# Moving weight casts and head gating to POOL, and reordering DVE, in the attention stage of a hybrid encoder step

## The chip, the cores and the metric

One core of one Trainium2 chip runs the whole program in a single launch. The metric is the device time of an execution in microseconds, lower is better. Times given for a kernel are the median of several runs; one further execution was taken with the hardware profiler, and every view quoted here is of that execution.

## The reference, cut to what matters

One layer of a streaming encoder works on 1024 prompt frames and 32 sample frames, which the kernel holds together as 1056 columns. The input is RMS-normed and multiplied by one wide matrix, from whose columns come queries, keys, values, forget logits, two gate paths and two mixing gates. Two branches follow and are merged:

```python
q, k, v, lf, ga, u, gb, ma, mb = mixer_inputs(xp, ...)      # one projection, split by columns
c = cumsum(lf)
# attention: 16 heads of 64, blocks of 128 queries
s = q @ k.T + c_q - c_k;  s = where(causal, s, min);  o = softmax(s) @ v
# convolution branch: depthwise width 31, LayerNorm over 1024 channels
conv = dwconv(u)
ya = (o * silu(ga)) @ w_pa
yb = (silu(layernorm(conv)) * silu(gb)) @ w_pb
m  = sigmoid(ma) * ya + sigmoid(mb) * yb
y  = x + m @ w_out
```

The sample frames do the same against a cache of 512 past frames.

## The kernel before, in words

**Stages.** The program goes through five stretches: the x split and first projections, the projections with the convolution running beside them, the attention, the two branch projections (pa, pb) and the output projection. This change lies in the attention. There PE does four kinds of work: the scores of a block, the transposes of the normalised weights P, the products with V, and, as filler between them, the remaining projections of the gates (gb, ma, mb).

**Numbers in halves.** A projection is made of three f16 products: the weight is cast to a high part `wh` (line 138) and a low part `wl` = raw - wh (line 141, three instructions of 3, 3 and 2 eighths of the weight), and the input likewise (`xh`, `xl`). Weights go in batches of two. Their jobs are hung on a counter of ticks: one tick is one step of a projection, three matmuls, and a projection has 24 ticks (8 k-tiles for each of 3 column chunks), so that a batch lasts 48. A batch's jobs, in ticks from the batch before it: squares for the scale (3, 13), the sum by PE (`total`, 25), the power of two (`power`, 27), the cast of each weight (`split`, 29 and 39) and its three low parts (`rest`, one, three and five ticks after the cast). A job that falls due is issued at that place in the engines' queues.

**Attention.** `seq` holds 132 items in order: 16 heads with 8 blocks of 128 queries (block i of a head sees (i+1) x 128 keys), and four `Sample` items. Step n of the main loop issues, in this order: the scores of item n+3 (`start`, which calls `scores`: PE products into `psS`, then on DVE the causal mask, line 1124, and the negated row maximum, line 1126); on some steps DMA loads of the next head; `turn` of item n (PE transposes P through `psT` banks, ACT copies the first four 128-wide pieces, DVE copies the rest when there are more than four, that is for blocks 4 to 7; both are line 1156); `soft` of item n+3 (ACT exponential with row sum, line 1133); `norm` of item n+2 (DVE reciprocal, line 1138, and POOL scaling of P, line 1139); filler ticks; `values` of item n-2 where it is due; filler ticks again. The second call of `values` that matters is at block 7: PE products with V (line 1172), ACT copies one half-row group (line 1176), DVE adds the other (line 1177), and for every second head DVE multiplies by the gate `ga` (line 1179), which a DMA brings (line 1161). The result goes to memory through SP (line 1181).

**Buffers.** `psS` has two buffers, so the scores of item n+3 wait for the exponential of item n+1. `psT` has two banks shared by transposes, value products, LayerNorm sums and the batch sums: a transpose waits until the copy of an earlier one has emptied a bank. `wh` and `wl` turn over three buffers, `raw` over four.

**Order.** In the attention the queues of PE, SP, DVE and ACT are as written in the program (`manual_schedule`); that of POOL is put in order by a planner with its own costs and due times.

**Fillers.** `fill(n)` issues n ticks of the remaining projections. Every step has two calls of `fill(2)`, but the first three blocks of head 8 have none. 22 projections, 528 ticks, are issued so. The LayerNorm statistics (`layernorm`) also run one piece a step once the convolution's sums are there, which in the profile is about head 8.

Of the kernel before, what the change touches and what calls it, by code (L numbers as in the profile page):

```python
# [8 lines left out]
F32 = mybir.dt.float32  # L9
# [5 lines left out]
ALU = mybir.AluOpType  # L15
# [38 lines left out]
def build(tc, xT, xt, wv, wf, ckT, cv, clT, stT, vec, cst, yT, kT, vO, lfO, cpT, csT):  # L54
# [35 lines left out]
    class Batch:  # L90
# [44 lines left out]
            nc.gpsimd.tensor_scalar(self.inv, q, back, 1.0, op0=ALU.mult, op1=ALU.mult)  # L135

        def high(self, i, wh, raw, ks):
            nc.scalar.mul(wh[:, ks, :], raw[:, ks, :], self.s[:, i:i + 1])  # L138

        def low(self, i, wl, wh, raw, ks):  # L140
# [80 lines left out]
    def begin():  # L221

        if not plan:
            return
        b = plan.pop(0)
        after = plan[0] if plan else None
        t = pace["tick"]
        jobs = [(25, b.total), (27, b.power)]
        if b.keys[0] == ("v", 0):
            jobs = [(32, b.total), (33, b.power), (10, lambda: b.stage(0)), (17, lambda: b.stage(1)),  # L230
                    (34, lambda: split.__setitem__(b.keys[0], split_v(0, b)))]
        elif b.n == 2:
            jobs += [(3, lambda: b.stage(0)), (13, lambda: b.stage(1))]
            for i, n in ((0, 29), (1, 39)):
                jobs.append((n, lambda i=i: b.split(i)))
                jobs += [(n + 1 + 2 * p, lambda i=i, p=p: b.rest(i, p)) for p in range(3)]
        else:
            jobs += [(3 + 10 * i, lambda i=i: b.stage(i)) for i in range(2)]
            jobs.append((29, lambda: split.__setitem__(b.keys[0], split_v(b.keys[0][1], b))))
        if after:  # L240
            jobs += [(5 + 10 * i, after.load) for i in range(after.n)]
        prep.extend((t + n, fn) for n, fn in sorted(jobs, key=lambda e: e[0]))
# [115 lines left out]
    def sums(f):  # L358
        return [lambda: from_shift(f, sides["y", f]), lambda: into_sums(f, sides["y", f])]
# [637 lines left out]
    pe = ExitStack()  # L997
    pe.enter_context(tc.manual_schedule(engines={E.PE, E.SP, E.DVE, E.Activation}))
    pace["rate"], pace["credit"] = R_A, 0.0
    taps.extend(sums(7))  # L1000
    psS = pool("psS", 2, stack=p2, space=PS)
    psT = pool("psT", 2, stack=p2, space=PS)
# [20 lines left out]
    def fill(n):  # L1023
        for _ in range(n):
            next(flow, None)

    class Sample:
# [15 lines left out]
        def scores(self):  # L1043
            g, kc, pf = self.g, self.kc, self.pf
            ps = psS.tile([128, 2, 512], F32, name="psS", tag="S")
            for j in range(4):
                rows = slice(64 * (j % 2), 64 * (j % 2) + 64)
                q = qs_t[rows, 2 * g + j // 2, :]
                nc.tensor.matmul(ps[32 * j:32 * j + 32, 0, :], q, kc[rows, j // 2, :], start=True, stop=True)
                nc.tensor.matmul(ps[32 * j:32 * j + 32, 1, :TS], q, ks_t[rows, 2 * g + j // 2, :],  # L1050
                                 start=True, stop=True)
            nc.vector.scalar_tensor_tensor(pf[:, :PAST], ps[:, 0, :], cq[:, g:g + 1], pf[:, :PAST],
                                           op0=ALU.add, op1=ALU.subtract)
# [50 lines left out]
    class Block:  # L1104
# [5 lines left out]
        def scores(self):  # L1110
            i = self.i
            QA, QB, KA, KB = self.head.q
            nk = (i + 1) * 128
            qsl = slice(i * 128, i * 128 + 128)
            ps = psS.tile([128, 2, 512], F32, name="psS", tag="S")
            nb = 1 if nk <= 512 else 2
            w = nk // nb
            wm = max(w, 256)
            for b in range(nb):
                ksl = slice(b * w, b * w + wm)  # L1120
                nc.tensor.matmul(ps[:, b, :wm], QB[:, qsl], KB[:, ksl], start=True, stop=False)  # L1121
                nc.tensor.matmul(ps[:, b, :wm], QA[:, qsl], KA[:, ksl], start=False, stop=True)  # L1122
            diag = ps[:, nb - 1, w - 128:w]
            nc.vector.tensor_add(diag, diag, cmask)  # L1124
            nm = ap.tile([128, 3], F32, name="nm", tag="nm", bufs=6)
            nc.vector.tensor_reduce(nm[:, 0:1], ps[:, :nb, :w], axis=AX.XY, op=ALU.max, negate=True)  # L1126
            self.at = ps, nm, nk, nb, w
# [30 lines left out]
        def values(self):  # L1158
            if self.i == 5 and self.head.h % 2:
                self.head.g = ap.tile([128, T], F32, name="ga", tag="kc", bufs=1)  # L1160
                nc.sync.dma_start(self.head.g, s_g["ga"][self.head.h // 2, :, :T])
            if self.i < 7:
                return
            e, V, ot, parts = self.head.h % 2, self.head.V, self.head.ot, self.head.p
            own = slice(64 * e, 64 * e + 64)
            oth = slice(64 - 64 * e, 128 - 64 * e)
            pos = [psT.tile([128, 512], F32, name="po", tag="T") for _ in range(2)]
            for c in range(4):
                po = pos[c // 2][:, 256 * (c % 2):256 * (c % 2) + 256]
                for j in range(2 * c + 2):  # L1170
                    rows = slice(64 * (j % 2), 64 * (j % 2) + 64)
                    nc.tensor.matmul(po[rows], V[:, j, :], parts[c][:, j, :], start=(c % 2 == 0 and j < 2),  # L1172
                                     stop=(c % 2 == 1 and j >= 2 * c))
            for u in range(2):
                sl = slice(512 * u, 512 * u + 512)
                nc.scalar.copy(ot[own, sl], pos[u][oth])
                nc.vector.tensor_add(ot[own, sl], ot[own, sl], pos[u][own])
                if e == 1:
                    nc.vector.tensor_mul(ot[:, sl], ot[:, sl], self.head.g[:, sl])
            if e == 1:  # L1180
                nc.sync.dma_start(s_o[self.head.h // 2, :, :T], ot)

# [23 lines left out]
    def layernorm():  # L1206

        shift = sides["shift"]
        for _ in range(4):
            yield  # L1210
        yield from over_channels(mean, lambda sl, ps: nc.scalar.mul(mean[:, sl], ps, 1.0 / D))

        def put(sl, ps):
            t = t352("t", 3)
            nc.scalar.activation(t, mean[:, sl], AF.Square)
            nc.vector.scalar_tensor_tensor(rstd[:, sl], ps, 1.0 / D, t, op0=ALU.mult, op1=ALU.subtract)
            nc.vector.tensor_add(mean[:, sl], mean[:, sl], shift[:, sl])
            nc.vector.tensor_scalar(rstd[:, sl], rstd[:, sl], EPS, None, op0=ALU.add)

        yield from over_channels(rstd, put)  # L1220
# [16 lines left out]
    heads[1].load()  # L1237
    for n in range(3):
        start(seq[n])
        seq[n].soft()  # L1240
        if n:
            seq[n - 1].norm()
        fill((8, 4, 0)[n])
    for n, b in enumerate(seq):
        if n + 3 < len(seq):
            start(seq[n + 3])
        if n + 9 < len(seq) and getattr(seq[n + 9], "i", 1) == 0:
            seq[n + 9].head.load()
        if n + 6 < len(seq) and isinstance(seq[n + 6], Sample):
            seq[n + 6].load()  # L1250
        if getattr(b, "i", 0) == 3 and b.head.h + 1 < H:
            heads[b.head.h + 1].load_v()
        b.turn()
        if n + 3 < len(seq):
            seq[n + 3].soft()
        if n + 2 < len(seq):
            seq[n + 2].norm()
        some = 2 if isinstance(b, Sample) or b.i > 2 or b.head.h != 8 else 0
        fill(some)
        if n >= 2 and pending(seq[n - 2]):  # L1260
            seq[n - 2].values()
        fill(some)
        if n >= 3 and isinstance(seq[n - 3], Sample):
            seq[n - 3].finish()
        if "ready" in sides:
            next(ln, None)
# [402 lines left out]
```

## Time and profile before

| what | value |
|---|---|
| time, median of 3 runs | 1348.63 us (1346.65 to 1349.82) |
| the profiled execution: its own time | 1345.89 us |
| the profiled execution: span from first to last instruction | 1344.1 us |
| busy share of the span: PE, DVE, ACT, POOL | 98%, 74%, 53%, 38% |
| chain that ended last: PE, DVE, ACT, issue, DMA | 82%, 9%, 3%, 2%, 2% |
| granted TensorE clock, mean | 0.996 |

A busy PE is a modelled quantity: matmuls overlap, so a row's duration is longer than the distance to the next one. A stall of PE therefore shows only where it is longer than the overlap. A wait is put down to the instruction whose signal came last. The page cuts the span into stretches by time; the attention lies from about 570 to 1055 us.

### The profile page before, as it was taken

What the parts mean: (1) busy time and instruction counts of PE and PEld (TensorE: products, weight loads), DVE (VectorE), ACT (ScalarE), POOL (GpSimd) and SP (SyncE); (2) the same over time, 40 slices, a digit from 0 to 9 for tenths busy, and PEclk for the clock granted to TensorE, in tenths of its full rate; (3) what the DMA queues carried; (4) which work ended last, traced back from release to release, by engine and by line L of the source; (5) the groups of instructions that cost most, each with busy time, mean ns of one, the idle gap of its engine ahead of it and who ended that gap; (6) DMA issues with size and microseconds to landing.
All of it is one profiled execution on the core that took longest, in us unless ns stands there. A gap on an engine that the chain in (4) does not pass through costs nothing.

```text
span 1344.1 us, 24837 instructions
## 1 busy us (share of the span) xinstructions
PE 1312.6 (98%) x9383; PEld 1003.1 (75%) x9383; DVE 990.4 (74%) x1532; ACT 719.0 (53%) x1362; POOL 505.8 (38%) x548
## 2 busy tenths in 40 slices
PE   8999999999999999999889998999999999999999
PEld 5687876666666666667567766777776699999998
DVE  6797879888999997987778866655554489166664
ACT  6644555757676743455555555655555566233320
POOL 2001124547484820243433442222222158255562
PEclk8999999999999999999999999999999999999999
DMA  6343233425352463535644643565452698544462
GB/s 251 98 140 104 93 112 118 139 82 187 95 180 87 162 166 109 160 90 155 165 109 123 186 132 99 147 179 132 131 152 54 240 313 262 176 128 146 142 190 69
DMA packets 113496, 194.97 MB, mean 145 GB/s; under 512 B 34080, under 2 KB 80032, under 8 KB 113376
## 3 DMA queue, kind: packets, MB, share of 16 engines
q1 hardware_dynamic: 113232, 193.31, 46.9%
q8 instruction: 74, 1.21, 0.4%
q14 instruction: 46, 0.38, 0.1%
q10 hardware_dynamic: 144, 0.07, 0.0%
HBM read 127.68 MB, written 65.64 MB: 144 GB/s over the span
## 4 chain that ended last, share of the span: by engine, by line
PE 82%; DVE 9%; ACT 3%; issue 2%; DMA 2%; SPq 1%; POOL 0%; DVEq 0%; ACTq 0%; POOLq 0%
PE pj L183 56%; PE pjv L761 6%; PE pj L1501 6%; PE po L1172 4%; PE ptr L1153 3%; DVE nm L1126 2%; DVE wl L141 2%; DVE y L371 2%; PE psS L1122 2%; PE psS L1121 2%; DMA ga<-s_ga 2%; ACT wh L138 1%; DVE psS L1124 1%; DMA s_q<-qh 1%; PE warm L477 1%
## 5 line engine op out<-in xcount | busy, mean ns | idle before, releaser
L183 PE MATMUL pj<-xh,wh 128*128 128x352 f16 (+2 forms) x1536 | 481.6, 314 | 2.3 <-ACT wh L138 1.4
L183 PE MATMUL pj<-xh,wl 128*128 128x352 f16 (+2 forms) x1536 | 481.2, 313 | 0.7 <-DVE wl L141 0.6
L183 PE MATMUL pj<-xl,wh 128*128 128x352 f16 (+2 forms) x1536 | 480.9, 313 | 0.5 <-DVE xl L579 0.4
L183 PEld LDWEIGHTS <-wh 128*128 128x128 f16 x3072 | 301.5, 98 | 162.1 <-issue 7.1
L371 DVE SCALAR_TENSOR_TENSOR y<-u,vec_t,y 128x1086 f32<-128x1086 f32 x240 | 346.8, 1446 | 12.0 <-ACT y L368 8.9
L1139 POOL TENSOR_SCALAR P<-P,nm 128x128 f32<-128x128 f32 (+7 forms) x128 | 129.9, 1015 | 279.9 <-DVE nm L1138 229.8
L183 PEld LDWEIGHTS <-wl 128*128 128x128 f16 x1536 | 150.5, 98 | 72.0 <-DVE wl L141 1.6
L141 DVE SCALAR_TENSOR_TENSOR wl<-raw,sc,wh 128x384 f16<-128x384 f32 (+1 forms) x192 | 128.2, 693 | 48.3 <-ACT wh L138 48.3
L1133 ACT ACTIVATE P<-psS,nm 128x128 f32<-128x128 f32 (+7 forms) x128 | 95.1, 743 | 113.3 <-DVE nm L1138 70.9
L1126 DVE TENSOR_REDUCE nm<-psS 128x1 f32<-128x128 f32 (+7 forms) x128 | 97.0, 758 | 12.5
L1153 PE MATMUL ptr<-ident,P 128*128 128x128 f32 x576 | 88.6, 276 | 17.3 <-DVE pt L1156 9.2
L175 POOL TENSOR_TENSOR wl<-raw,wh 128x384 fp32r<-128x384 f32 (+1 forms) x51 | 63.3, 1270 | 74.3 <-ACT wh L172 58.6
L1153 PEld LDWEIGHTS ptr<-ident,P 128*128 128x128 f32 x576 | 69.2, 141 | 28.2 <-DVE pt L1156 12.1
L1156 ACT COPY pt<-ptr 128x512 f32<-128x512 f32 (+3 forms) x128 | 64.3, 502 | 44.4 <-PE ptr L1153 43.2
L1121 PE MATMUL psS<-KB,QB 128*128 128x256 f32 (+2 forms) x192 | 81.8, 427 | 0.6 <-ACT P L1133 0.6
L880 POOL TENSOR_TENSOR sql<-sqf,sqh 128x352 fp32r<-128x352 f32 x48 | 57.0, 1187 | 65.8 <-ACT sqh L877 65.8
L138 ACT ACTIVATE wh<-raw,sc 128x1024 f16<-128x1024 f32 (+1 forms) x68 | 73.9, 1091 | 8.2 <-DVE sc L158 7.9
L1172 PE MATMUL po<-pt,V 128*64 128x256 f32 x640 | 72.8, 382 | 2.5 <-ACT pts L1078 1.7
L1124 DVE TENSOR_TENSOR psS<-psS,cmask 128x128 f32<-128x128 f32 x128 | 37.6, 294 | 46.0 <-PE psS L1122 45.6
L906 POOL TENSOR_TENSOR ql<-qn,qh 128x352 fp32r<-128x352 f32 (+1 forms) x48 | 67.8, 1429 | 6.6 <-ACT qh L905 6.5
L761 PE MATMUL pjv<-vwh,xh 128*128 128x260 f16 x256 | 70.1, 274 | 0.0
L761 PE MATMUL pjv<-vwl,xh 128*128 128x260 f16 x256 | 70.0, 273 | 0.0
(271 smaller groups left out, 2532.9 us busy)
## 6 DMA issues: line engine op xcount, KB each, us to landing
raw<-wf SPq DMA_DIRECT2D x92, 512.0 KB
QB<-s_q SPq DMA_DIRECT2D x32, 256.0 KB
KB<-s_k SPq DMA_DIRECT2D x32, 256.0 KB
kT<-qn SPq DMA_DIRECT2D x8, 528.0 KB
s_ga<-t SPq DMA_DIRECT2D x24, 176.0 KB
s_gb<-t SPq DMA_DIRECT2D x24, 176.0 KB
s_ma<-t SPq DMA_DIRECT2D x24, 176.0 KB
s_mb<-t SPq DMA_DIRECT2D x24, 176.0 KB
```

The costliest lines, as they stand in the source:

```text
L138: nc.scalar.mul(wh[:, ks, :], raw[:, ks, :], self.s[:, i:i + 1])
L141: nc.vector.scalar_tensor_tensor(wl[:, ks, :], raw[:, ks, :], self.s[:, i:i + 1], wh[:, ks, :], op0=ALU.mult, op1=ALU.subtract)
L183: nc.tensor.matmul(ps, a[:, kt, :], b(kt, sl), start=(first and n == 0), stop=(last and n == N - 1))
L371: t = nc.vector.scalar_tensor_tensor(y, u[:, i:i + CW], w, y, op0=ALU.mult, op1=ALU.add)
L761: nc.tensor.matmul(ps[:, :VC], a, b, start=(n == 0), stop=(n == 23))
L1121: nc.tensor.matmul(ps[:, b, :wm], QB[:, qsl], KB[:, ksl], start=True, stop=False)
L1126: nc.vector.tensor_reduce(nm[:, 0:1], ps[:, :nb, :w], axis=AX.XY, op=ALU.max, negate=True)
L1133: nc.scalar.activation(P[:, :nk].rearrange("p (b w) -> p b w", b=nb), ps[:, :nb, :w], AF.Exp, bias=nm[:, 0:1], accum_out=nm[:, 1:2])
L1139: nc.gpsimd.tensor_scalar(P[:, :nk], P[:, :nk], nm[:, 2:3], 1.0, op0=ALU.mult, op1=ALU.mult)
L1153: nc.tensor.transpose(pt[:, 128 * j:128 * j + 128], P[:, 128 * (4 * u + j):128 * (4 * u + j) + 128], ident)
L1172: nc.tensor.matmul(po[rows], V[:, j, :], parts[c][:, j, :], start=(c % 2 == 0 and j < 2), stop=(c % 2 == 1 and j >= 2 * c))
L1501: nc.tensor.matmul(pss[c][:, :HC], a[:, k, :], x, start=(not more and kt == 0 and n == 0), stop=(kt == 3 and n == 2), skip_group_check=more)
```

## The change

- While the attention runs, the cast of a weight to `wh` is a POOL `tensor_scalar` instead of an ACT `mul`. A batch begun there has its sum at tick 23 (was 25), its power at 24 (27), its casts at 25 and 34 (29 and 39), and its low parts 6, 8 and 10 ticks behind the cast (was 1, 3 and 5), which puts them at 31, 33, 35 and 40, 42, 44 (was 30, 32, 34 and 40, 42, 44).
- `scores` issues the PE products alone. The mask and the maximum are in a new method `top`, which the main loop calls after `turn`, ahead of `soft`. So DVE's copy of the turned P is issued ahead of the mask and maximum of the item three further on. Sample items are split the same way.
- The product with the gate `ga` is issued on POOL instead of DVE.
- In LayerNorm the ACT square of the mean's chunk is issued one step ahead of the matmul and the DVE work that uses it.
- The first three blocks of head 8 get filler ticks like all others; block 6 of heads 2 to 13 gets three ticks in place of four. The sum of ticks stays 528.

```diff
         def high(self, i, wh, raw, ks):
+            if sides.get("cast") == "pool":
+                nc.gpsimd.tensor_scalar(wh[:, ks, :], raw[:, ks, :], self.s[:, i:i + 1], 1.0, op0=ALU.mult, op1=ALU.mult)
+                return
             nc.scalar.mul(wh[:, ks, :], raw[:, ks, :], self.s[:, i:i + 1])
...
         elif b.n == 2:
             jobs += [(3, lambda: b.stage(0)), (13, lambda: b.stage(1))]
-            for i, n in ((0, 29), (1, 39)):
+            lag = 6 if sides.get("cast") == "pool" else 1
+            for i, n in ((0, 29), (1, 39)) if lag == 1 else ((0, 25), (1, 34)):
                 jobs.append((n, lambda i=i: b.split(i)))
-                jobs += [(n + 1 + 2 * p, lambda i=i, p=p: b.rest(i, p)) for p in range(3)]
+                jobs += [(n + lag + 2 * p, lambda i=i, p=p: b.rest(i, p)) for p in range(3)]
+            if lag > 1:
+                jobs[:2] = [(23, b.total), (24, b.power)]
...
     pace["rate"], pace["credit"] = R_A, 0.0
+    sides["cast"] = "pool"
...
+        def top(self):
+            ps, nk, nb, w = self.at
             diag = ps[:, nb - 1, w - 128:w]
             nc.vector.tensor_add(diag, diag, cmask)
...
                 if e == 1:
-                    nc.vector.tensor_mul(ot[:, sl], ot[:, sl], self.head.g[:, sl])
+                    nc.gpsimd.tensor_mul(ot[:, sl], ot[:, sl], self.head.g[:, sl])
...
-        def put(sl, ps):
+        for c in range(3):
+            sl = csl(c)
             t = t352("t", 3)
             nc.scalar.activation(t, mean[:, sl], AF.Square)
-            nc.vector.scalar_tensor_tensor(rstd[:, sl], ps, 1.0 / D, t, op0=ALU.mult, op1=ALU.subtract)
+            yield
+            pm = psT.tile([128, 512], F32, name="psn", tag="T")
+            nc.tensor.matmul(pm[:, :CH], ones_f, rstd[:, sl], start=True, stop=True)
+            nc.vector.scalar_tensor_tensor(rstd[:, sl], pm[:, :CH], 1.0 / D, t, op0=ALU.mult, op1=ALU.subtract)
...
         b.turn()
         if n + 3 < len(seq):
+            seq[n + 3].top()
             seq[n + 3].soft()
         if n + 2 < len(seq):
             seq[n + 2].norm()
-        some = 2 if isinstance(b, Sample) or b.i > 2 or b.head.h != 8 else 0
-        fill(some)
+        fill(2)
         if n >= 2 and pending(seq[n - 2]):
             seq[n - 2].values()
-        fill(some)
+        fill(1 if getattr(b, "i", 0) == 6 and 2 <= b.head.h < 14 else 2)
```

More of the change, by code (lines that the diff above doesn't have):

```diff
@@ L1051, in scores @@
                                  start=True, stop=True)
+            self.ps = ps
+        def top(self):
+            g, ps, pf = self.g, self.ps, self.pf
             nc.vector.scalar_tensor_tensor(pf[:, :PAST], ps[:, 0, :], cq[:, g:g + 1], pf[:, :PAST],
@@ L1122, in scores, with top @@
                 nc.tensor.matmul(ps[:, b, :wm], QA[:, qsl], KA[:, ksl], start=False, stop=True)
+            self.at = ps, nk, nb, w
+        def top(self):
+            ps, nk, nb, w = self.at
             diag = ps[:, nb - 1, w - 128:w]
@@ L1211, in layernorm @@
         yield from over_channels(mean, lambda sl, ps: nc.scalar.mul(mean[:, sl], ps, 1.0 / D))
-        def put(sl, ps):
+        for c in range(3):
+            sl = csl(c)
             t = t352("t", 3)
             nc.scalar.activation(t, mean[:, sl], AF.Square)
-            nc.vector.scalar_tensor_tensor(rstd[:, sl], ps, 1.0 / D, t, op0=ALU.mult, op1=ALU.subtract)
+            yield
+            pm = psT.tile([128, 512], F32, name="psn", tag="T")
+            nc.tensor.matmul(pm[:, :CH], ones_f, rstd[:, sl], start=True, stop=True)
+            nc.vector.scalar_tensor_tensor(rstd[:, sl], pm[:, :CH], 1.0 / D, t, op0=ALU.mult, op1=ALU.subtract)
             nc.vector.tensor_add(mean[:, sl], mean[:, sl], shift[:, sl])
             nc.vector.tensor_scalar(rstd[:, sl], rstd[:, sl], EPS, None, op0=ALU.add)
-        yield from over_channels(rstd, put)
         for c in range(6):
@@ L1239, in build @@
         start(seq[n])
+        seq[n].top()
         seq[n].soft()
```

## The prediction

> **What bounds the kernel now.** I read the stages by window first, then PE's waits in the attention, then what DVE waits for there, then the timeline around a few stalls.
>
> ```profile
> core 0: us, PE busy (x) PEld busy (x) DVE busy (x) ACT busy (x) POOL busy (x), PEclk, DMA share, GB/s
> 46.00:570.00 524.00, 523.17 (x3750) 363.86 (x3749) 461.81 (x529) 305.60 (x564) 193.31 (x192) 1.00 0.41 130
> 800.00:850.00 50.00, 45.26 (x296) 32.70 (x296) 31.97 (x80) 28.61 (x69) 12.23 (x21) 0.97 0.48 117
> 1055.00:1255.00 200.00, 200.00 (x1266) 193.48 (x1265) 119.69 (x133) 88.39 (x116) 104.94 (x77) 1.00 0.64 213
> 570.00:1055.00 485.00, 463.86 (x3447) 335.10 (x3446) 321.92 (x694) 272.83 (x590) 155.12 (x218) 1.00 0.48 130
> ```
>
> PE is full before the attention (523.17 of 524 us) and after it (200.00 of 200), so only the attention has room: 485.00 - 463.86 = 21.1 us of idle PE. DVE is busy for 321.92 of the 485 us, ACT for 272.83, POOL for 155.12; none is the bound by its work. Who ended PE's idle time:
>
> ```profile
> PE ptr L1153 <- DVE pt L1156: 9.2, 11, 1.7
> PE ptr L1153 <- ACT pt L1156: 6.4, 5, 2.2
> PE po L1172 <- ACT pts L1078: 1.7, 2, 0.9
> PE ptr L1153 <- DVE ot L1177: 1.2, 1, 1.2
> PE po L1172 <- ACT mean L1211: 0.7, 1, 0.7
> PE psS L1121 <- ACT P L1133: 0.6, 2, 0.4
> PE psn L1202 <- ACT pt L1156: 0.6, 1, 0.6
> ```
>
> The columns are us in total, times, the longest. They sum to 20.4 us, nearly all of the idle time, and nearly all is one thing: a transpose waits for a bank of psT that DVE or ACT has not emptied. Both queues are first in, first out, so the question is what stood ahead of the copy. Two stalls:
>
> ```profile
> 648.41 1.22 DVE L1126 TENSOR_REDUCE nm<-psS 128x1 f32<-128x1024 f32 x1
> 649.55 0.28 DVE L1156 COPY pt<-ptr 128x128 f32<-128x128 f32 x1
> 649.89 0.44 PE L1153 MATMUL ptr<-ident,P 128*128 128x128 f32 x2 [1.16 <-DVE pt L1156]
> ```
>
> ```profile
> 679.16 1.14 ACT L138 ACTIVATE wh<-raw,sc 128x1024 f16<-128x1024 f32 x1
> 680.21 0.54 ACT L944 ACTIVATE t<-pj,sc 128x352 f32<-128x352 f32 x1
> 680.34 0.62 DVE L141 SCALAR_TENSOR_TENSOR wl<-raw,sc,wh 128x384 f16<-128x384 f32 x1 [2.19 <-ACT wh L138]
> 680.73 0.58 ACT L1156 COPY pt<-ptr 128x512 f32<-128x512 f32 x1
> 681.37 0.33 PE L1153 MATMUL ptr<-ident,P 128*128 128x128 f32 x1 [1.05 <-ACT pt L1156]
> ```
>
> In the first, a copy of 0.28 us stands behind a maximum of 1.22 us that nobody needs for another step. In the second, ACT's copy stands behind a weight cast of 1.14 us, and DVE meanwhile stood 2.19 us at the low part, which waits for that cast. DVE's own waits say how often:
>
> ```profile
> DVE psS L1124 <- PE psS L1122: 45.6, 48, 2.3
> DVE wl L141 <- ACT wh L138: 32.5, 20, 2.2
> DVE ot L1179 <- DMA ga<-s_ga: 9.9, 6, 3.3
> ```
>
> 20 waits for a cast and 6 for the gate's DMA, 42.4 us, are idle time of DVE with copies and maxima queued behind it.
>
> **The change part by part.** Rows for the prices:
>
> ```profile
> L138 ACT ACTIVATE wh<-raw,sc 128x1024 f16<-128x1024 f32 x22 | 25.1, 1140 | 0.0
> L1179 DVE TENSOR_TENSOR ot<-ot,ga 128x512 f32<-128x512 f32 x16 | 11.1, 693 | 10.2 <-DMA ga<-s_ga 9.9
> L1139 POOL TENSOR_SCALAR P<-P,nm 128x1024 f32<-128x1024 f32 x16 | 21.1, 1317 | 14.7 <-DVE nm L1138 9.9 <-ACT P L1133 4.5
> L175 POOL TENSOR_TENSOR wl<-raw,wh 128x384 fp32r<-128x384 f32 x34 | 45.3, 1354 | 74.3 <-ACT wh L172 58.6 <-issue 15.4 <-POOL ml L1421 0.2
> L351 POOL TENSOR_TENSOR rstd<-rstd,y 128x1024 f32<-128x1024 f32 x7 | 19.0, 2720 | 20.3 <-ACT y L355 20.3
> L371 DVE SCALAR_TENSOR_TENSOR y<-u,vec_t,y 128x1086 f32<-128x1086 f32 x46 | 64.0, 1391 | 2.3 <-ACT y L368 2.2
> L141 DVE SCALAR_TENSOR_TENSOR wl<-raw,sc,wh 128x384 f16<-128x384 f32 (+1 forms) x67 | 39.1, 605 | 32.5 <-ACT wh L138 32.5
> ```
>
> and from the waits and the timeline, with the taps of the first 170 us of the attention by window:
>
> ```profile
> 570.00:740.00 170.00, 49.26 (x35) 1.00 0.47 127
> PEld ptr L1153 <- POOL P L1139: 2.0, 4, 1.2
> 715.49 1.33 DVE L371 SCALAR_TENSOR_TENSOR y<-u,vec_t,y 128x1086 f32<-128x1086 f32 x1
> 715.67 2.14 POOL L1139 TENSOR_SCALAR P<-P,nm 128x1024 f32<-128x1024 f32 x1
> 838.79 1.12 POOL L1139 TENSOR_SCALAR P<-P,nm 128x1024 f32<-128x1024 f32 x1 [0.30 <-DVE nm L1138]
> 836.98 1.52 POOL L1139 TENSOR_SCALAR P<-P,nm 128x896 f32<-128x896 f32 x1 [5.12 <-DVE nm L1138]
> 839.15 0.93 PE L1153 MATMUL ptr<-ident,P 128*128 128x128 f32 x7
> ```
>
> *Casts to POOL, low parts six ticks behind.* ACT loses 22 x 1.14 = 25.1 us. POOL gains 22 instructions of a kind whose nearest row is the scaling of P, also 1024 wide and one tensor in, 1.317 us in the mean: 29 us. No row here writes f16 from POOL, so I keep the ends of the timeline rows, 1.12 and 2.14 us: 25 to 47 us. A batch of 48 ticks is 12 steps of four ticks, about 12 x 485/132 = 44 us, so six ticks are about 5.5 us, over twice the dearer cast; the low parts find it done and DVE's 32.5 us go. On PE this is the ACT row: the copies that wait behind a cast. I take 5 of its 6.4 us; the rest stood behind squares and evacuations that stay.
>
> *Mask and maximum behind the copy.* Only steps that turn blocks 4 to 7 have a DVE copy, so 64 steps change. The copy is then first in line, and 8 of the 9.2 us go (the rest stood behind taps and low parts, which stay). The added wait: the maximum now waits for a copy that waits for up to eight transposes. Seven take 0.93 us (row at 839.15) and the copy 0.28, so the maximum, the exponential on ACT behind it and the reciprocal come about 1.2 us later where DVE was idle, nothing where it was late. They are needed two steps on, about 2 x 485/132 = 7 us, so I cost this at nothing in the sum and keep what it takes from P's margin for the rivals.
>
> *Gate on POOL.* DVE loses 16 x 0.693 = 11.1 us and the 9.9 us of DMA wait. POOL gets 16 products with two tensors in: between 1.354 us for 384 columns and 2.720 for 1024, by the line through both 1.63 us at 512, together 26 us, plus the same DMA wait. What is queued behind on POOL is the next scaling of P. On PE the "DVE ot" row, 1.2 us, goes; the store of `ot` comes some 2 us later, with nothing waiting for it but a buffer two heads on.
>
> *Squares ahead, fillers spread.* Twelve ticks of three matmuls go to head 8:
>
> ```profile
> 491.34 21.50 PE pj L183 x144
> 827.39 0.50 PE L183 MATMUL pj<-xh,wh 128*128 128x352 f16 x1
> 837.12 0.31 PE L183 MATMUL pj<-xh,wh 128*128 128x352 f16 x1
> ```
>
> At 21.50/144 = 0.149 us each that is 12 x 3 x 0.149 = 5.4 us of PE work into a place where PE stood, taken from steps where it did not: the same work, but the LayerNorm waits (0.7 and 0.6 us) are covered. Around 827 us the same matmul took 0.50 us where it takes 0.31 ten us later, and the window 800 to 850 has a clock of 0.97: 0.03 x 50 = 1.5 us, which goes if PE does not thin out there. Each removed wait also hides 0.31 - 0.149 = 0.16 us of a matmul's modelled tail; some 16 waits, 2.6 us.
>
> *New costs.* POOL's three sources together go from 155 to about 155 + 29 + 26 = 210 of 485 us, and its order is a planner's. The weight loads of transposes wait for POOL 2.0 us today. I let that double, and 0.6 us for DVE: 2.6 us. Its ends are 0, if POOL's idle time takes everything, and the 33 us of the slower rival.
>
> **Sum.** 8 + 5 + 1.2 + 1.3 + 1.5 + 2.6 - 2.6 = 17 us. Against the profiled execution: 1345.9 - 17 = 1328.9. That execution lies 2.7 us below the median of the runs, so on their scale 1348.6 - 17 = **1331.6 us**. The most that can go is 21.1 us idle, 1.5 of clock and some 4 of tails (26 waits x 0.16), 27 us: 1322. By a third to a half of the terms missing, 9 us: 1340.
>
> **The rivals.** *The port eats DVE's gain.* At 715.67 the scaling of P started 0.18 us into a tap and took 2.14 us, against 1.12 alone: the two exclude each other. Taps and low parts, 64.0 + 39.1 us of DVE's time, are the instructions with two tensors in. If the 55 us added on POOL held DVE for their whole length, DVE would be as late as with the 32.5 + 9.9 + 11.1 = 53.5 us it gets rid of, and the 8 and 1.2 us would stay lost. Left are 5 + 1.3 + 1.5 and 1 of tails, less 2: 7 us, 1341.6 (1337 to 1346). Against it: the taps end early (35 of the 46 lie before 740 us, 49.26 of 64.0 us), and 103.1 of 485 us of DVE's time, a fifth, is of this kind. The Trainium skill, "SBUF — State Buffer", section "Who interferes with whom", says that a DVE instruction with two SBUF inputs and a GpSimd one that reads SBUF share a port that is locked for the whole instruction, the later one fully blocked; by that rule every such meeting costs the loser its whole wait, and the time would lean to this rival's 1341.6. The rows at 715 agree.
>
> *POOL becomes late (slower).* POOL is in order. Block 6's scaling ended at 836.98 + 1.52 = 838.50 and its transposes began at 839.15: 0.65 us to spare. A cast of 2.14 us ahead of such a scaling costs PE 1.5 us; at all 22 casts 33 us, less the 17: +16, 1364.6. It breaks even when 17/1.5 = 11 of the casts stand before a tight block. For it: POOL's order is a planner's, gate products wait there for DMA, and the later reciprocal takes from the same margin. Against it: POOL idles most of the stage, and a cast is issued behind the scaling of its own step.
>
> *One wait for another (no change).* The maximum is up to 1.2 us later, so the exponential is, and ACT's copy of the next block stands behind the exponential: the 17 us come back as waits for ACT, 1348.6 (1346 to 1351). Against it: ACT has 25.1 us less to do, and had only 273 of 485.
>
> **How the numbers follow.** Forecast 0.64 (1324 to 1340), the port 0.16, POOL late 0.12, no change 0.08. A measurement of this kernel tells 0.2%, 2.7 us. Faster: the forecast and the port, 0.80; same 0.08; slower 0.12. The range runs from 1322, where all is won, to 1350, which leaves out the slower case and little else (some 0.15 above, 0.05 below).
>
> **What would show it.** Right: PE's idle time in the attention falls from 21 us to 4 to 8, "DVE wl <- ACT wh" is gone, the DVE copies' row of PE's waits falls under 2 us, and no clock below 0.99 stands in a window about head 8. POOL's cast takes 1.1 to 2.1 us, its gate product 1.3 to 2.7. Wrong: transposes wait for "POOL P" by more than 5 us (POOL late); low parts and taps grow well above 0.605 and 1.391 us with the copies still late (the port); "ACT pt" grows above 6.4 us (one wait for another).

## Result and the profile after

The changed kernel takes **1331.7 us** in the median (1330.78 to 1332.38), the kernel before 1347.64 us (1345.03 to 1349.82) beside it: ratio 0.9869, 95% interval 0.9851 to 0.9888, or 17.7 us less. The profiled execution took 1331.66 us (span 1329.8, mean clock 0.997).

The attention by window, after, with the stretch about head 8, in the same columns as before:

```profile
800.00:850.00 50.00, 49.97 (x347) 36.06 (x346) 31.45 (x81) 27.83 (x66) 19.74 (x30) 1.00 0.54 140
570.00:1038.00 468.00, 458.29 (x3436) 333.68 (x3434) 315.41 (x678) 248.48 (x568) 211.95 (x254) 1.00 0.50 135
```

The attention now ends at about 1038 us, and PE idles 468.00 - 458.29 = 9.7 us in it, where it idled 21.1. The stretch about head 8 is full (49.97 of 50 us, clock 1.00). By the first and the last instruction of the attention in the chain, the stage went from 482.4 us (570.23 to 1052.64) to 466.8 (571.27 to 1038.09): 15.6 us less. What lies before it took 1.0 us longer and what lies behind it 0.2, so the whole gain is in the attention. The two profiled executions differ by 14.2 us (1345.89 - 1331.66), less than the medians, as that of before lay below its median.

PE's waits there, after (us in total, times, the longest):

```profile
PE po L1187 <- ACT pts L1089: 2.6, 2, 1.8
PE ptr L1168 <- ACT pt L1171: 2.4, 2, 1.7
PE ptr L1168 <- DVE pt L1171: 1.7, 2, 1.4
PE ptr L1168 <- DVE os_t L1113: 1.5, 2, 1.2
PE ptr L1168 <- POOL P L1154: 1.1, 3, 0.6
...
```

The two rows of the turned copies, 9.2 and 6.4 us before, are 1.7 and 2.4 now. Three rows grew: `pts`, which belongs to the four Sample items, `os_t` and POOL's scaling of P; the last two were not in the list.

The queues that changed hands, after: DVE's wait for the cast, and the weight loads that wait for POOL.

```profile
DVE wl L144 <- POOL wh L139: 0.3, 1, 0.3
PEld ptr L1168 <- POOL P L1154: 3.5, 5, 1.5
```

And the two moved operations (count, busy us, mean ns, and POOL's idle time ahead of them with what ended it):

```profile
L139 POOL TENSOR_SCALAR wh<-raw,sc 128x1024 f16<-128x1024 f32 x22 | 24.5, 1126 | 0.0
L1194 POOL TENSOR_TENSOR ot<-ot,ga 128x512 f32<-128x512 f32 x16 | 21.7, 1358 | 32.5 <-DMA ga<-s_ga 15.2 <-DVE ot L1192 14.2 <-issue 3.1
```

DVE's 32.5 us behind the cast are gone (0.3). The gate's DMA wait did not go away: it moved to POOL, where it is longer (15.2 us) and costs PE little: transposes wait 1.1 us for POOL's scaling of P, their weight loads 3.5 us (2.0 before).

### The profile page after: what moved, and what is told of

The parts are those of the page before. It is cut to its first block, busy times and chain, and to the rows that moved or that the text cites. A ratio compares the mean times of both kernels' runs of the same rounds, so it can differ in the third digit from the quotient of the medians.

```text
span 1329.8 us, 24806 instructions
## 1 busy us (share of the span) xinstructions
PE 1308.3 (98%) x9383; PEld 1002.7 (75%) x9383; DVE 979.6 (74%) x1516; ACT 695.2 (52%) x1340; POOL 559.4 (42%) x586
## 4 chain that ended last, share of the span: by engine, by line
PE 89%; DVE 5%; ACT 2%; issue 1%; POOL 1%; DMA 1%; SPq 1%; DVEq 0%; POOLq 0%; ACTq 0%
PE pj L186 60%; PE pjv L767 6%; PE pj L1519 6%; PE po L1187 5%; PE ptr L1168 4%; PE psS L1133 2%; PE psS L1132 2%; DVE wl L144 1%; DVE y L377 1%; DMA s_y<-y 1%; PE pst L866 0%; DVE nm L1141 0%; PE pst L867 0%; DMA ga<-s_ga 0%; PE ptx L582 0%
## 5 line engine op out<-in xcount | busy, mean ns | idle before, releaser
L1154 POOL TENSOR_SCALAR P<-P,nm 128x128 f32<-128x128 f32 (+7 forms) x128 | 143.8, 1124 | 195.2 <-DVE nm L1153 171.6
L144 DVE SCALAR_TENSOR_TENSOR wl<-raw,sc,wh 128x384 f16<-128x384 f32 (+1 forms) x192 | 133.3, 718 | 16.3 <-ACT wh L141 15.8
L178 POOL TENSOR_TENSOR wl<-raw,wh 128x384 fp32r<-128x384 f32 (+1 forms) x51 | 59.6, 1196 | 61.0 <-ACT wh L175 46.4
L120 POOL CAST topb<-tops 128x2 bf16<-128x2 f32 x35 | 19.0, 541 | 137.0 <-ACT junk L117 87.1
L767 PE MATMUL pjv<-vwh,xl 128*128 128x260 f16 x256 | 69.9, 273 | 0.0
```

The costliest lines, as they stand in the source:

```text
L144: nc.vector.scalar_tensor_tensor(wl[:, ks, :], raw[:, ks, :], self.s[:, i:i + 1], wh[:, ks, :], op0=ALU.mult, op1=ALU.subtract)
L767: nc.tensor.matmul(ps[:, :VC], a, b, start=(n == 0), stop=(n == 23))
L1154: nc.gpsimd.tensor_scalar(P[:, :nk], P[:, :nk], nm[:, 2:3], 1.0, op0=ALU.mult, op1=ALU.mult)
```

## Experiments

The total agreed with the sum, but a total of four parts can agree by errors that cancel. So each part was run alone, then the whole was run without one part, and then came the questions that these raised. Ratios are to the kernel before, run on the same chip.

| kernel | median us | ratio, 95% interval | difference, us |
|---|---|---|---|
| after, all four parts | 1331.70 | 0.9869 (0.9851 to 0.9888) | -17.7 |
| casts on POOL and new ticks, alone | 1339.04 | 0.9918 (0.9904 to 0.9932) | -11.1 |
| new ticks alone, casts stay on ACT | 1338.33 | 0.9909 (0.9890 to 0.9929) | -12.3 |
| mask and maximum behind the copy, alone | 1352.54 | 1.0019 (1.0007 to 1.0030) | +2.6 |
| gate on POOL, alone | 1344.20 | 0.9962 (0.9947 to 0.9976) | -5.1 |
| fillers and squares, alone | 1346.45 | 0.9966 (0.9951 to 0.9981) | -4.6 |
| after without the reordering | 1334.71 | 0.9886 (0.9868 to 0.9904) | -15.4 |
| after with the casts on ACT | 1331.89 | 0.9870 (0.9857 to 0.9883) | -17.6 |
| after without the gate on POOL | 1341.36 | 0.9925 (0.9905 to 0.9946) | -10.1 |
| after, each cast made twice | 1338.80 | 0.9922 (0.9907 to 0.9938) | -10.5 |
| after, Sample's large copies on DVE | 1334.20 | 0.9885 (0.9867 to 0.9904) | -15.5 |
| after, Sample's copies exchanged | 1332.14 | 0.9865 (0.9844 to 0.9886) | -18.2 |
| the same with the casts on ACT | 1336.57 | 0.9891 (0.9871 to 0.9911) | -14.7 |

A difference is the ratio less one times the median of before in that comparison (1347.64 to 1350.73).

**Casts on POOL with the new ticks, alone.**

```diff
+    sides["cast"] = "pool"          # with high() and the ticks of the change
     # scores calls top() itself; gate on DVE; fillers and LayerNorm as before
```

> Of the change only the casts on POOL with the new ticks; everything else as before. Separate terms (the prediction's): the cast was worth ACT's share, about 5 us and 0.8 of tails, less POOL's cost: 4 us faster, ratio 0.997, and PE's row for DVE's copies stays near 9.2 us. One cause, shared lateness: the casts' waits, 32.5 us of DVE, were what made DVE late at the copies too, so this part alone takes 8 to 11 us, ratio 0.992 to 0.994, and the row for DVE's copies falls below 5 us.

It gave 11.1 us, more than twice the 5 in the sum. PE's waits for DVE's and ACT's copies in it:

```profile
PE ptr L1170 <- DVE pt L1173: 5.8, 7, 1.5
PE ptr L1170 <- ACT pt L1173: 3.4, 2, 2.4
```

The ACT row fell by 3.0 us, and the DVE row, which the sum had left to the reordering, by 3.4: low parts that no longer stand waiting let the copies behind them pass. Together that is 6.4 us. The two profiled executions differ by 1345.89 - 1339.26 = 6.6 us, so the rows cover what the traces can show; the execution of before lies 3.8 us below the median of its runs here, and the 11.1 us rest on the medians.

**Mask and maximum behind the copy, alone.**

```diff
         b.turn()
         if n + 3 < len(seq):
+            seq[n + 3].top()        # taken out of scores
             seq[n + 3].soft()
```

> Only the mask and maximum behind the turned copy. Separate terms: 8 us of the copies' row and 1.6 of tails, ratio 0.993, with the row for DVE's copies under 2 us. Shared lateness: the copy is still behind a low part that waits for its cast, so at most 4 us, ratio 0.997 or above, and the row stays above 4 us.

It is 2.6 us slower, and the interval leaves out no change; neither expectation had a loss. PE's waits in the attention, the largest rows:

```profile
PE ptr L1167 <- ACT pt L1170: 7.4, 7, 2.2
PE ptr L1167 <- DVE pt L1170: 5.7, 4, 3.5
PE po L1186 <- ACT pts L1088: 2.7, 2, 1.8
PE ptr L1167 <- POOL P L1153: 1.6, 3, 0.7
PE po L1186 <- ACT pt L1170: 1.3, 2, 0.7
...
PE psS L1131 <- ACT P L1147: 1.2, 2, 0.8
```

The DVE row fell by 3.5 us, although 3.5 of what is left are a single stall of another kind (last section): of the kind that was to go, 2.2 us remain. But the two rows of ACT's copies, that of `pts`, that of P's scaling on POOL and that of the scores' buffers grew together from 6.4 + 1.7 + 0.6 = 8.7 us to 14.2.

Where this comes from is seen by the width of the exponential, which tells the step. The order on DVE changes only where the turned block is one of 4 to 7, and the exponential three items on then has 1024, 128, 256 or 384 columns (but for some steps beside the Sample items). ACT's idle time ahead of the exponentials of 384 and of 512 columns, in this kernel, then in the kernel before:

```profile
L1147 ACT ACTIVATE P<-psS,nm 128x384 f32<-128x384 f32 x16 | 9.3, 581 | 19.3 <-DVE nm L1152 19.3
L1147 ACT ACTIVATE P<-psS,nm 128x512 f32<-128x512 f32 x16 | 11.0, 686 | 16.1 <-DVE nm L1152 16.1
```

```profile
L1133 ACT ACTIVATE P<-psS,nm 128x384 f32<-128x384 f32 x16 | 9.3, 581 | 8.9 <-DVE nm L1138 5.6 <-DVE nm L1126 2.9
L1133 ACT ACTIVATE P<-psS,nm 128x512 f32<-128x512 f32 x16 | 11.0, 686 | 16.5 <-DVE nm L1138 16.5
```

Over the four widths whose order changed, it went from 47.3 to 76.5 us; over the four others, from 66.0 to 63.6. One such step and what followed, in this kernel and in the kernel before:

```profile
725.17 0.69 DVE L1170 COPY pt<-ptr 128x512 f32<-128x512 f32 x1
726.17 0.56 DVE L1140 TENSOR_REDUCE nm<-psS 128x1 f32<-128x384 f32 x1
726.85 0.58 ACT L1147 ACTIVATE P<-psS,nm 128x384 f32<-128x384 f32 x1 [1.53 <-DVE nm L1152]
727.42 1.14 ACT L141 ACTIVATE wh<-raw,sc 128x1024 f16<-128x1024 f32 x1
728.59 1.15 DVE L144 SCALAR_TENSOR_TENSOR wl<-raw,sc,wh 128x384 f16<-128x384 f32 x2 [1.79 <-ACT wh L141]
732.77 0.36 ACT L1170 COPY pt<-ptr 128x256 f32<-128x256 f32 x1
733.19 3.24 PE L1186 MATMUL po<-pt,V 128*64 128x256 f32 x28 [0.75 <-ACT pt L1170]
```

```profile
720.13 0.56 DVE L1126 TENSOR_REDUCE nm<-psS 128x1 f32<-128x384 f32 x1
720.60 0.69 DVE L1156 COPY pt<-ptr 128x512 f32<-128x512 f32 x1
720.80 0.58 ACT L1133 ACTIVATE P<-psS,nm 128x384 f32<-128x384 f32 x1
721.38 1.14 ACT L138 ACTIVATE wh<-raw,sc 128x1024 f16<-128x1024 f32 x1
722.55 1.15 DVE L141 SCALAR_TENSOR_TENSOR wl<-raw,sc,wh 128x384 f16<-128x384 f32 x2 [1.19 <-ACT wh L138]
726.73 0.36 ACT L1156 COPY pt<-ptr 128x256 f32<-128x256 f32 x1
```

DVE's copy starts 4.57 us later here than before, as do PE's transposes ahead of it; so late is the whole kernel at this place. From the exponential on, everything is 6.0 us later, 1.5 us more: the exponential idles 1.53 us for the maximum that now stands behind the copy, the weight cast on ACT stands behind the exponential, DVE's low parts wait for the cast, and ACT's copy two steps on is late, so that PE stands 0.75 us, where it does not stand before. The rival *one wait for another* is right for this part: it gives back most of what it wins. The stall of the last section, which the kernel before does not have, is of the size of the whole loss, so that the part by itself may be about even.

**Gate on POOL, alone.**

```diff
-                    nc.vector.tensor_mul(ot[:, sl], ot[:, sl], self.head.g[:, sl])
+                    nc.gpsimd.tensor_mul(ot[:, sl], ot[:, sl], self.head.g[:, sl])
```

> Only the gate product on POOL. Separate terms: 1.2 to 1.5 us, ratio 0.999. Shared lateness: the gate's DMA wait, 9.9 us of DVE, also made later copies late, 3 to 4 us, ratio 0.997.

5.1 us, where the sum had 1.2. PE's wait for DVE's copies is 8.0 us (9.2 before), and the row "DVE ot" of 1.2 us is gone. These are 2.4 us. Between the profiled executions the gain is no more than 1345.89 - 1343.92 = 2.0 us, which they cover; that it is 5.1 rests on the medians, and no trace shows the rest.

**Fillers and squares, alone.**

```diff
-        fill(some)
+        fill(2)
...
-        fill(some)
+        fill(1 if getattr(b, "i", 0) == 6 and 2 <= b.head.h < 14 else 2)
```

with the LayerNorm square one step ahead, as in the change.

> Only the fillers spread and the squares a step ahead. Separate terms: 1.3 us of waits, 1.5 of clock and 0.3 of tails, 3 us, ratio 0.998, with no stretch of half clock near head 8. Shared lateness: the waits about head 8 come from the gate's DMA and a cast, which stay, so the clock's 1.5 us at most, ratio 0.999 to 1.

4.6 us by the medians, more than either expectation; the sum had 1.3 for waits and 1.5 for the clock, and some of the tails. The stretch about head 8 in it has a clock of 1.00 (0.97 before), and PE is busy for 48.95 of 50 us (45.26 before):

```profile
800.00:850.00 50.00, 48.95 (x365) 35.65 (x364) 30.64 (x77) 31.84 (x71) 14.62 (x23) 1.00 0.44 121
```

But the runs of this kernel lie between 1341.02 and 1349.75 us, and the profiled one was the slowest of them. Over the attention PE idles no less in it than before (485.00 - 463.11 = 21.9 us), as the waits for DVE's copies grew from 9.2 us, by the stall of the last section (3.3 us) and by others, to 13.7. What the part is worth in time thus rests on the medians alone.

The four parts alone come to -11.1 + 2.6 - 5.1 - 4.6 = -18.2 us, the whole to -17.7: they nearly add up, one of them with the wrong sign.

**The whole without the reordering.**

```diff
+            self.top()              # at the end of scores, as before
...
-            seq[n + 3].top()
```

> The whole change except that mask and maximum stay ahead of the turned copy. Against the whole change at 0.9869. If the reorder is worth nothing or a little harm wherever it stands, as alone (1.0019): 0.985 to 0.987. If it pays once DVE no longer waits for casts and the gate, because then DVE is on time and the maximum is all that stands ahead of the copy: 0.990 to 0.993, with the row for DVE's copies at 5 us or more.

15.4 us are left of 17.7, between the two expectations, so in company the reordering gains some 2 us; the intervals overlap (0.9868 to 0.9904 against 0.9851 to 0.9888), and its sign there is not settled. The row for DVE's copies is 8.3 us, as the second expectation had it; 3.3 us of it are the stall of the last section, so the reordering takes this row from 5.0 us to the 1.7 of the whole change. In company, too, the exponentials of the four widths wait longer with it (72.7 us against 41.3 here), but PE's wait for ACT's copies does not grow by it (2.4 us in both), only that for `pts` (2.6 against 1.0). Why not was not tested; that the low parts no longer stand right behind a cast would break the chain seen above.

**The whole with the casts on ACT, at the new ticks.**

```diff
-            if sides.get("cast") == "pool":
-                nc.gpsimd.tensor_scalar(wh[:, ks, :], ...)
-                return
             nc.scalar.mul(wh[:, ks, :], raw[:, ks, :], self.s[:, i:i + 1])
```

> The whole change with its new ticks, but the casts stay on ACT: the low parts still come six ticks behind. If the gain of the cast's part is DVE's wait for it (32.5 us), the place of the cast hardly matters: 0.987 to 0.989. If it is ACT's 25.1 us ahead of the copies: 0.992 to 0.994, with ACT's row of PE's waits at 6 us or more.

No difference to the whole (0.9870 against 0.9869). PE's waits for the copies:

```profile
PE ptr L1165 <- ACT pt L1168: 3.0, 3, 1.7
PE ptr L1165 <- DVE pt L1168: 2.2, 3, 1.3
```

So what the part gains is not ACT's 25 us of casts. Neither of the two traces has the long stall of the last section, which makes this the cleanest comparison of all. The next run asks the same of the part by itself.

**The new ticks alone.** Casts stay on ACT, and nothing else of the change is made.

```diff
-            for i, n in ((0, 29), (1, 39)):
+            for i, n in ((0, 25), (1, 34)):
                 jobs.append((n, lambda i=i: b.split(i)))
-                jobs += [(n + 1 + 2 * p, lambda i=i, p=p: b.rest(i, p)) for p in range(3)]
+                jobs += [(n + 6 + 2 * p, lambda i=i, p=p: b.rest(i, p)) for p in range(3)]
+            jobs[:2] = [(23, b.total), (24, b.power)]
```

> Of the change only the new ticks: the casts stay on ACT, a step earlier, and the low parts come six ticks behind; all else as before. If DVE's wait for the cast is the whole worth of that part: as the casts on POOL alone, 0.991 to 0.993, with no wait of low parts for casts. If ACT's time counts too: 0.994 to 0.996.

12.3 us, as with the casts moved (11.1, intervals 0.9890 to 0.9929 and 0.9904 to 0.9932). DVE's wait for the cast is gone, and PE's waits for the copies fell as with the casts on POOL (DVE's from 9.2 to 4.8 us, ACT's from 6.4 to 3.7).

The engine that casts does not matter here; the six ticks between cast and low part do. They come from the cast, which is issued four and five ticks earlier (25 and 34 in place of 29 and 39): the low parts themselves stand at most one tick later than before. The sum and the power moved with the cast, by two and three ticks, and were not tried apart. As 3.1 of the 4.8 us are the stall of the last section, which the run with the casts on POOL does not have, some us of difference between the two could be hidden.

**The whole with every cast made twice on POOL.** The second writes the same values again.

```diff
                 nc.gpsimd.tensor_scalar(wh[:, ks, :], raw[:, ks, :], self.s[:, i:i + 1], 1.0, ...)
+                nc.gpsimd.tensor_scalar(wh[:, ks, :], raw[:, ks, :], self.s[:, i:i + 1], 1.0, ...)
```

> The whole change with every cast made twice on POOL (the second writes the same values), 22 more instructions of 1.13 us, 24.8 us. If POOL has room and the port costs little: within 1.5 us of the whole change, 0.987 to 0.988. If POOL's queue is near its limit, or the port holds DVE: half or more of the 24.8 us shows, 0.994 to 1.005, with PE's waits for POOL above 6 us (queue) or low parts well above 0.64 us (port).

The second casts took 28.4 us on POOL and cost 1338.80 - 1331.70 = 7 us, between the two expectations. PE's waits for POOL, and the low parts with their mean duration:

```profile
PE ptr L1169 <- POOL P L1155: 3.4, 2, 2.3
```

```profile
L145 DVE SCALAR_TENSOR_TENSOR wl<-raw,sc,wh 128x384 f16<-128x384 f32 (+1 forms) x67 | 47.5, 726 | 4.1 <-POOL wh L140 4.0
```

Low parts take 0.726 us (0.641 with single casts), and transposes wait for POOL 3.4 us (1.1); PE's wait for DVE's copies is 3.8 us, of which 3.5 are the stall of the last section. By the estimate given there, that stall is worth some 4 of the 7 us. Both rivals about POOL begin to show, then, at one load more than the change puts on it, and are worth some 3 us.

**The whole without the gate on POOL.**

```diff
-                    nc.gpsimd.tensor_mul(ot[:, sl], ot[:, sl], self.head.g[:, sl])
+                    nc.vector.tensor_mul(ot[:, sl], ot[:, sl], self.head.g[:, sl])
```

> The whole change except that the gate product stays on DVE. If the parts add as they did alone (gate 0.9962): 0.990 to 0.991, with DVE waiting some 10 us for the gate's DMA. If the gate's wait harmed only a DVE that casts had made late: 0.987 to 0.988.

Without it 17.7 us become 10.1, so it seems to be worth 7.6 in company, more than either expectation had. DVE's wait for the gate:

```profile
DVE ot L1194 <- DMA ga<-s_ga: 17.4, 7, 3.2
```

Once DVE no longer stands at the casts, it stands longer at the gate's DMA (17.4 us, 9.9 before). PE's wait for DVE's copies is 4.9 us (1.7 in the whole change). But of these, 3.5 are one stall, with which the last section deals, so 7.6 is not all the gate's own; by the estimate given there some 4 us of it are that stall.

**Can the rest be had?** Of the four largest rows of PE's waits in the changed kernel, two are the Sample's, `pts` and `os_t`. Three versions exchange the engines of these copies. First, the large `pts` copy and both `os_t` copies on DVE:

```diff
-            nc.scalar.copy(pts[:, 0:4, :], ...)
+            nc.vector.tensor_copy(pts[:, 0:4, :], ...)
-            nc.scalar.copy(os_t[0:64, ...], p4[:, :, 0, :])
+            nc.vector.tensor_copy(os_t[0:64, ...], p4[:, :, 0, :])
```

> The whole change, and for the four Sample items the large copy of the turned weights and both copies of the result on DVE instead of ACT (and half on ACT). What is left of PE's waits there, 2.6 us behind ACT's squares and 1.5 us behind a copy that waits for ACT's on the same tile, should go: 3 to 4 us, 0.984. If DVE is then late elsewhere: 0.987, no change.

No gain (1334.20). Second, both `pts` copies on DVE, both `os_t` copies on ACT, and `power` due in the tick of `total`:

```diff
-                jobs[:2] = [(23, b.total), (24, b.power)]
+                jobs[:2] = [(23, b.total), (23, b.power)]
...
-            nc.scalar.copy(pts[:, 0:4, :], ...)
+            nc.vector.tensor_copy(pts[:, 0:4, :], ...)
...
-            nc.scalar.copy(pts[:TS, 4, :], pt[:TS, :128])
+            nc.vector.tensor_copy(pts[:TS, 4, :], pt[:TS, :128])
...
-            nc.vector.tensor_copy(os_t[64:128, ...], p4[:, :, 1, :])
+            nc.scalar.copy(os_t[64:128, ...], p4[:, :, 1, :])
```

> The whole change, with both copies of a Sample's turned weights on DVE, both copies of its result on ACT, and the power of two in the same tick as the sum, so that no turn stands between them with only one bank. Of PE's waits that are left, 2.6 us behind ACT's squares, 1.5 us at the result's copies and 1.7 us at about 889 us should go: 4 to 5 us, ratio 0.983 to 0.984. If each only gives way to another wait: 0.987.

Third, the second with the casts on ACT:

> The same version with the casts on ACT instead of POOL. As the whole change with casts on ACT equalled the one with casts on POOL: within 1.5 us of that version, 0.983 to 0.985. If POOL's queue is what is left: 2 us faster; if ACT's copies are: 2 us slower.

The second equals the whole change (1332.14), the third is 4.4 us above the second, and its trace has the long stall of the last section. In the second the `pts` wait only changed its engine, and grew (2.6 us behind ACT, 3.7 behind DVE).

None of the three beats the changed kernel by more than its interval.

## Why the prediction was right, and where it was not

The total held: 17 us forecast, 17.7 measured by medians (14.2 between the profiled executions, 15.6 in the attention alone). The shares did not, and their errors cancelled, so that the fit is in part luck: the term of 8 us gave -2.6 alone and some 2 in company, and the term of 5 gave 11.

- *Only the attention has room; the idle time of PE is what can go.* Right: the other stages moved by 1.0 and 0.2 us. PE's idle time fell to 9.7 us, where 4 to 8 were named. With 11.4 us less of idle time in 15.6 us, 4.2 are left for clock and tails, as the sum had it (1.5 + 2.6); the tails are only this difference, not measured.
- *Reordering, 8 us.* This is the step that failed. The copies did come sooner, nearly as priced: DVE's row fell by 9.2 - 2.2 = 7.0 us of the kind that was meant. The failure is the added wait, which was costed at nothing because the exponential is needed only two steps on. ACT's queue is in order too, and a weight cast and the copies of the next blocks stand behind that exponential: its waits grew by 29.2 us, and the rows of PE that hang on ACT and on P by 5.5. Alone the part ended 2.6 us slower, with a stall of another kind of that size in its trace; in company it is worth some 2 us, of unsettled sign. The step should have asked what stands behind the instruction that is made late, not only when its result is needed. In the whole change the DVE row of 1.7 us is under the 2 that the prediction named as its proof, so that sign by itself would have confirmed a wrong step.
- *Casts off ACT, 5 us.* Mis-sized, and by the wrong cause: 11.1 us measured alone, 12.3 with the casts still on ACT. The prediction quoted DVE's 32.5 us at the cast and let them go, but gave the saving no value on PE beyond ACT's row. Those 32.5 us were the term that counts, as even the ACT row fell by 2.7 us with the casts still on ACT (3.0 with them on POOL): the low part came one tick (some 0.9 us, 44/48) behind a cast of 1.14 us that has a queue of its own ahead of it, and DVE stood still with copies and maxima queued behind. That the low parts would find the cast done six ticks later was right (0.3 us).
- *Gate, 1.2 us.* Too small: 5.1 alone. The price was the "DVE ot" row only; another 1.2 us came off DVE's copies, which stand behind the 9.9 us of DVE's wait for the DMA. The other 2.7 us show in no trace; the two profiled executions differ by 2.0 us only.
- *Fillers, LayerNorm, clock, 1.3 + 1.5 and a share of the tails.* 4.6 us by the medians, with no trace that shows it; the clock in 800 to 850 went to 1.00 as named.
- *New costs, 2.6 us.* Somewhat small, and partly elsewhere: weight loads wait for POOL 1.5 us more, as named; of PE's own rows `os_t` (1.5), POOL's scaling (1.1) and `pts` (0.9 more) are new or grew, 3.5 us.
- *The prices on POOL.* The cast took 1.126 us (1.1 to 2.1 named, at its lower end), the gate product 1.358 (1.3 to 2.7; the line through two other rows had given 1.63).
- *The port.* Taps and low parts after:

```profile
L377 DVE SCALAR_TENSOR_TENSOR y<-u,vec_t,y 128x1086 f32<-128x1086 f32 x47 | 67.9, 1446 | 2.3 <-ACT y L374 2.2
L144 DVE SCALAR_TENSOR_TENSOR wl<-raw,sc,wh 128x384 f16<-128x384 f32 (+1 forms) x67 | 41.8, 641 | 0.4 <-POOL wh L139 0.3
```

  They grew by 4% and 6%, 55 and 36 ns each. The rival needed 55 us; it took some 67.9 - 64.0 - 1.4 (one tap more in the stretch) + 41.8 - 39.1 = 5.2. By the rule of the Trainium skill that the prediction cites ("SBUF — State Buffer", "Who interferes with whom") each meeting is lost in full; in one meeting of the last section a tap grew by 0.64 us where the scaling had 0.84 us left to run, so that most of it was lost. But the meetings were few. What the prediction did not ask is who loses. POOL's scalings of P, before and after:

```profile
L1139 POOL TENSOR_SCALAR P<-P,nm 128x128 f32<-128x128 f32 (+7 forms) x128 | 129.9, 1015 | 279.9 <-DVE nm L1138 229.8 <-ACT P L1133 22.0 <-DVE sc L157 19.3
L1154 POOL TENSOR_SCALAR P<-P,nm 128x128 f32<-128x128 f32 (+7 forms) x128 | 143.8, 1124 | 195.2 <-DVE nm L1153 171.6 <-DVE sc L160 10.3 <-PE pj L186 7.9
```

  The same 128 scalings took 13.9 us more on POOL, against some 5 more on DVE. POOL had the room for it; that all of it comes from such meetings is not shown.
- *POOL late.* Not at 22 casts (the row of waits for P is 1.1 us); at 44 it begins, with 3.4 us there.

## What to carry to other kernels

In an in-order queue, the price of a wait is what stands behind the waiting instruction: a consumer issued right behind its producer on another engine cost 32.5 us of DVE and, by the medians, some 12 us of time here, and issuing the producer four to five ticks earlier, with the consumer left almost where it was, won that back with no engine changed. When an instruction is moved back in its queue, follow its consumer into the consumer's queue and ask what stands behind it there. And a total that fits its forecast proves none of its parts: run each alone, above all the one on which the sum rests most.

## What the runs showed of the hardware

**One meeting of DVE and POOL, with two outcomes, is worth some 4 us.** Where the first Sample runs, a tap and a low part on DVE meet POOL's scaling of P and the LayerNorm addition to `rstd`. After, on DVE, POOL and PE (start, duration, in brackets the wait ahead of it):

```profile
642.07 1.35 DVE L377 SCALAR_TENSOR_TENSOR y<-u,vec_t,y 128x1086 f32<-128x1086 f32 x1
643.33 1.05 DVE L144 SCALAR_TENSOR_TENSOR wl<-raw,sc,wh 128x256 f16<-128x256 f32 x1
641.83 2.27 POOL L1154 TENSOR_SCALAR P<-P,nm 128x768 f32<-128x768 f32 x1 [3.67 <-DVE nm L1153]
644.08 3.76 POOL L357 TENSOR_TENSOR rstd<-rstd,y 128x1024 f32<-128x1024 f32 x2
644.73 0.85 PE L1168 MATMUL ptr<-ident,P 128*128 128x128 f32 x6 [1.35 <-DVE pt L1171]
```

The same place in the whole without the gate on POOL:

```profile
644.50 1.99 DVE L377 SCALAR_TENSOR_TENSOR y<-u,vec_t,y 128x1086 f32<-128x1086 f32 x1
646.41 2.56 DVE L144 SCALAR_TENSOR_TENSOR wl<-raw,sc,wh 128x256 f16<-128x256 f32 x1
644.25 1.09 POOL L1154 TENSOR_SCALAR P<-P,nm 128x768 f32<-128x768 f32 x1 [4.74 <-DVE nm L1153]
646.27 2.80 POOL L357 TENSOR_TENSOR rstd<-rstd,y 128x1024 f32<-128x1024 f32 x2 [0.92 <-ACT y L361]
649.31 1.51 PE L1168 MATMUL ptr<-ident,P 128*128 128x128 f32 x6 [3.51 <-DVE pt L1171]
```

In the first, POOL's scaling is held (2.27 us for 768 columns, 1.09 in the second) and PE stands 1.35 us. In the second the tap (1.99 us against 1.35) and the low part (2.56 against 1.05) are held, the copy behind them is late, and PE stands 3.51 us. What decides is not seen in the trace: the scaling is recorded 0.24 us ahead of the tap in the first and 0.25 in the second, so that the order of the recorded starts does not tell which will be held.

All fourteen traces show one of the two outcomes here. POOL is held in the kernel before, in the changed one, in the runs of the casts and of the gate alone, in the whole with the casts on ACT, and in the first two Sample versions. DVE is held, and PE stands 3.1 to 3.5 us, in the seven others: the reordering, the fillers and the new ticks alone, the whole without the reordering, without the gate on POOL and with double casts, and the last Sample version. In all these seven the clock of the window 640 to 660 is 0.83 or 0.91; in the other seven it is 1.00, but for the casts alone with 0.83. An estimate of the price from the two kernels shown is 3.51 - 1.35 = 2.2 us of stall and 0.09 x 20 = 1.8 us of clock, 4 us in all. So where only one of two kernels has the long stall, their difference in the table can carry some 4 us of it: the reordering, the fillers and the new ticks alone, what the gate is worth in company (7.6 us), the double casts (7) and the last two versions (4.4). Only one execution of each kernel has a trace, so whether a kernel always falls the same way is open. Moving that addition off POOL was not tried.

**The clock can fall after a stall of 1.7 us.** The window 640 to 660, which holds this place, has a clock of 1.00 with the shorter of the two stalls shown above and of 0.91 with the longer one. But a stall's length does not decide alone. About 889 us, after and the first Sample version have the same stall of 1.73 us; after keeps its clock, the other loses it:

```profile
886.00:896.00 10.00, 8.28 (x59) 5.94 (x58) 7.18 (x20) 4.12 (x12) 3.74 (x6) 1.00 0.28 73
```

```profile
886.00:896.00 10.00, 8.27 (x48) 5.69 (x46) 4.95 (x16) 3.26 (x9) 3.60 (x5) 0.83 0.29 83
```

Inside that window the clock of the other is at 0.50 for some 3.4 us:

```profile
890.00:891.00 1.00, 1.00 (x5) 0.51 (x4) 0.90 (x4) 0.00 (x0) 0.00 (x0) 0.50 0.00 0
```

By the mean of 0.83 that costs 10 x 0.17 = 1.7 us. The Trainium skill, "TensorE: Matmul & The Clock Gate", section "HAM oscillation — how this bites in real kernels", gives as the rule that PE should have no idle gap over some 3.4 us. These rows differ: 1.73 us of idle time within a thin stretch were enough in one execution, and not in another. What decides between the two, the runs here leave open.
